# An edge tile of 672 bytes and the forgetting attention's two heads side by side, in a three-layer network

## The chip, the cores and the metric

One core of one Trainium2 chip runs the whole network in one launch. The metric is device time in microseconds, the median of three runs.

## The reference

512 tokens of width 1024 in float32 go through three layers. Layer one mixes with an RWKV recurrence, layer two with a gated convolution of 31 taps; both go on with cross attention to 256 memory tokens and with a feed-forward net with a short convolution (width 2 x 2816). Layer three is a hybrid of gated linear attention and forgetting attention, the part that the change rewrites:

```
h = rmsnorm_2(x, norm_mix_g)
gq, gk, gv, gr, glr, fq, fk, fv, ff, g_gla, g_fox = split(h @ w_in)
...
fqh, fkh = rmsnorm of fq, fk for each of 8 heads of 64
log_f = log_sigmoid(ff + fox_forget_b); c = cumsum(log_f over tokens)
for i in range(4):                       # query blocks of 128 tokens
    lo, hi = i * 128, (i + 1) * 128
    logits = q[lo:hi] @ k[:hi].T * 64**-0.5 + c[lo:hi, None] - c[None, :hi]
    p = softmax(where(causal, logits, -inf))
    out[lo:hi] = p @ v[:hi]
...
y = sigmoid(g_gla + gate_b[0]) * (o_gla @ w_gla_branch) + sigmoid(g_fox + gate_b[1]) * (o_fox @ w_fox_branch)
x = x + y @ w_out
```

## The kernel before

Activations stand with the 1024 channels on partitions, eight tiles of 128 x 512 tokens, float32. A dense product of float32 numbers is made from three float32r matmuls: weights and activations are split into a high part (rounded to float32r) and the rest, and `acc3` (L218 to L220) issues high x high, weight high x activation low, weight low x activation high for each of the 128-channel steps. An output tile of 128 channels x 512 tokens from 1024 input channels is so 24 matmuls of 512 columns, and one from 2816, as in the second product of a feed-forward net, 66: 24 from `bh` and `bl`, 24 from `h`, 18 from `mid`. The weights are read by SyncE's queue into `wr`, rounded by ScalarE into `wh` (L63) and the rest made by VectorE or GpSimd into `wl` (L64).

Tiles come from pools that the program lays out as two stacks in each partition of the on-chip memory. The left stack holds the weights, temporaries and the `home` tiles (`h0` and on, which hold `h` and, in the feed-forward nets, `mid`), and above them the pools of a stage. The right stack holds one pool, `act`, opened by `open_act` (L122 and on): `x` and the split activations `ah`, `al`, `bh`, `bl` (`slot`, `pair`), 2,048 bytes each. It begins at byte 229,344 and grows down. Pool `hy` of the hybrid stage begins with `aw2` and `fb` (L716), and all that this stage allocates later stands above.

In the hybrid stage the projections of forgetting attention for four pairs of heads, its attention itself and twenty output tiles of the two gates (`gates`, one tile being 24 float32r matmuls) are interleaved by hand. `fox_pair` (L945) is a generator; each `next` issues a step of the pair: the projection of q and k (L954, yields), the norms (L962 to L971, yields), then for each head the broadcast of its decay sums (L977 to L979), the scores of four query blocks (L984, on 64 rows of the array, since a head has 64 channels) with their softmax (L986 on VectorE, L988 on GpSimd, L990 on VectorE, L991 on ScalarE, L992 and L993 on VectorE), yields, then for each of four key blocks the transpositions of the probabilities (L1000), ScalarE's copy (L1003) and one value matmul over all the queries that see the key block (L1004, 64 output channels, 512 to 128 columns). A string for each pair, `FOX` (L1631), sets the order: `c` is the next step of the pair, `Q` the projection of the next pair, `n` the norms of the next pair, `G` one gate tile. Within its queue an engine runs in order; a scheduler places instructions by the program's text and dependences, and the engines wait for one another by semaphores. A float32 matmul, such as those of L984, L1000 or L1004, shows as two records in the trace unless it transposes.

Of the kernel before, what the change touches and what calls it, by code (L numbers as in the profile page):

```python
# [8 lines left out]
F32 = mybir.dt.float32  # L9
F32R = mybir.dt.float32r  # L10
AF = mybir.ActivationFunctionType
# [4 lines left out]
P = 128  # L16
T = 512
# [78 lines left out]
class Net:  # L96
    def __init__(self, ctx, tc, args, vec_at, order):
        self.ctx, self.tc, self.nc, self.a, self.vec_at = ctx, tc, tc.nc, args, vec_at
        nc = self.nc
        self.keep = ctx.enter_context(tc.tile_pool(name="keep", bufs=1))  # L100
        self.wpool = ctx.enter_context(tc.tile_pool(name="wts", bufs=1))
        self.tmp = ctx.enter_context(tc.tile_pool(name="tmp", bufs=1))
        self.hpool = ctx.enter_context(tc.tile_pool(name="home", bufs=1, reuse_waits="tile"))
        self.w = Weights(nc, self.wpool, [(k, self.wap(k)) for k in order])
        self.n = 0
        self.logs = False
        nv = args["vecs"].shape[1]
        self.vecs = self.keep.tile([P, nv], F32, name="vecs")
        self.consts()
# [597 lines left out]
    def hybrid(self, g_next):  # L707
        nc = self.nc
        mmul = nc.tensor.matmul
        with ExitStack() as ctx:  # L710
            pool = ctx.enter_context(self.tc.tile_pool(name="hy", bufs=1, reuse_waits="tile"))
            rs, rs_col = self.two_norms("final_g")
            xs, side = self.xs, self.side
            w2 = pool.tile([17, 256], F32, name="aw2")
            nc.sync.dma_start(out=w2, in_=self.a["gla_w2"])
            fb = pool.tile([P, 8], F32, name="fb")  # L716
            nc.sync.dma_start(out=fb, in_=self.a["fox_b"])

            def evict_rs(out, ps, n=T):
# [20 lines left out]
            with self.tc.tile_pool(name="hyt", bufs=1, reuse_waits="tile") as tp:  # L740
                self.chunk_consts(tp, True)

                ps = self.mm()
# [10 lines left out]
                for i in range(2):  # L754
                    ps = self.aux()
# [3 lines left out]
                    t = self.t512("u", 3)  # L759
# [14 lines left out]
                cq = pool.tile([P, 4, 8], F32, name="cq")  # L774
# [18 lines left out]
                for p in range(2):  # L793
# [10 lines left out]
                    ps = self.aux()  # L804
# [6 lines left out]
                for tb in range(4):  # L811
                    for p in range(2):
# [4 lines left out]
                        for h in range(2):  # L817
                            r = slice(h * 64, h * 64 + 64)
# [6 lines left out]
                            po = self.mm()  # L825
                            mmul(po[:, :P], lhsT=gv[tb][:, hh * P : (hh + 1) * P], rhs=sh, start=True, stop=(tb == 0), skip_group_check=True)
                            pos.append(po)
                        for c in range(2):
                            n = 2 * tb + c
                            if n:  # L830
                                for h in range(2):
                                    r = slice(h * 64, h * 64 + 64)
                                    o = c * 64
                                    mmul(pos[h][:, o : o + 64], lhsT=state[p][r, :], rhs=gqk[p][r, n * 64 : n * 64 + 64], start=False, stop=(c == 1),
                                         skip_group_check=True)
                            if n < 7:
                                kv = self.aux()
                                for h in range(2):
                                    r = slice(h * 64, h * 64 + 64)
                                    hh = 2 * p + h  # L840
                                    mmul(kv[r, :P], lhsT=kt[p][tb][c * 64 : c * 64 + 64, r], rhs=gv[tb][c * 64 : c * 64 + 64, hh * P : (hh + 1) * P],
                                         start=True, stop=True)
# [10 lines left out]
                ps = self.aux()  # L853
# [9 lines left out]
                for h in range(4):  # L863
                    b = self.bcast_tokens(y[:, :, h])
# [4 lines left out]
            with self.tc.tile_pool(name="hyf", bufs=1, reuse_waits="tile") as tp:  # L869
                fv = [tp.tile([P, 512], F32, name=f"fv{b}") for b in range(4)]  # L870
# [74 lines left out]
    def fox_pair(self, p, tp, xs, rs, cq, fv, of):  # L945
        nc = self.nc
        mmul = nc.tensor.matmul
        qk = {}

        def evict(m, ps):  # L950
            u = tp.tile([P, T], F32, tag="qk", bufs=4, name=self.nm("qk"))
            nc.vector.tensor_tensor(out=u, in0=ps, in1=rs, op=ALU.mult)
            qk[m // 4] = u

        self.linear("hy_fqk", KD, [p, 4 + p], lambda k: xs[k], evict, group=1)
        yield
        ps = self.aux()
        for i in range(2):
            s = self.t512("sq", 2)
            nc.scalar.activation(out=s, in_=qk[i], func=AF.Square)  # L960
            for tb in range(4):
                mmul(ps[:, tb * 4 + 2 * i : tb * 4 + 2 * i + 2], lhsT=s[:, tb * P : (tb + 1) * P], rhs=self.blk2, start=True, stop=True)  # L962
        v, y = self.small(16, "z"), self.small(16, "z")
        nc.vector.tensor_scalar(out=v, in0=ps[:, :16], scalar1=1.0 / 64, scalar2=1e-6, op0=ALU.mult, op1=ALU.add)
        self.rsqrt(y, v, 16)
        y4 = y.rearrange("p (a b) -> p a b", b=4)
        nc.vector.tensor_scalar(out=y4[:, :, 0:2], in0=y4[:, :, 0:2], scalar1=0.125, scalar2=None, op0=ALU.mult)
        rows = self.rows(y4, 4, tp)
        for i in range(2):
            b = self.pick(self.sel2, i, rows)  # L970
            nc.vector.scalar_tensor_tensor(out=qk[i], in0=qk[i], scalar=self.vec("fox_g", i), in1=b, op0=ALU.mult, op1=ALU.mult)  # L971
        yield
        po = None
        for h in range(2):
            hd = 2 * p + h
            r = slice(h * 64, h * 64 + 64)
            b = self.bcast_tokens(cq[:, :, hd])  # L977
            cb = tp.tile([P, T], F32, tag="cb", bufs=2, name=self.nm("cb"))
            nc.scalar.activation(out=cb, in_=b, func=AF.Copy)  # L979
            es = []  # L980
            for qb in range(4):
                n = (qb + 1) * P
                ps = self.aux()
                mmul(ps[:, :n], lhsT=qk[0][r, qb * P : n], rhs=qk[1][r, :n], start=True, stop=True)  # L984
                e = tp.tile([P, T], F32, tag="fe", bufs=4, name=self.nm("fe"))
                nc.vector.scalar_tensor_tensor(out=e[:, :n], in0=ps[:, :n], scalar=cq[:, qb, hd : hd + 1], in1=cb[:, :n], op0=ALU.add, op1=ALU.subtract)  # L986
                d = e[:, qb * P : n]
                nc.gpsimd.affine_select(out=d, in_=d, compare_op=ALU.is_ge, fill=-3.0e38, base=0, pattern=[[-1, P]], channel_multiplier=1)  # L988
                nm, sm = self.small(1, "c"), self.small(1, "c")
                nc.vector.tensor_reduce(out=nm, in_=e[:, :n], axis=AX.X, op=ALU.max, negate=True)  # L990
                self.last_exp = nc.scalar.activation(out=e[:, :n], in_=e[:, :n], func=AF.Exp, bias=nm, accum_out=sm).ins  # L991
                nc.vector.reciprocal(out=sm, in_=sm)  # L992
                nc.vector.tensor_scalar(out=e[:, :n], in0=e[:, :n], scalar1=sm, scalar2=None, op0=ALU.mult)  # L993
                es.append(e)
            yield
            po = po or self.mm()
            for kb in range(4):
                ps = self.aux()
                for qb in range(kb, 4):
                    nc.tensor.transpose(ps[:, (qb - kb) * P : (qb - kb + 1) * P], es[qb][:, kb * P : (kb + 1) * P], self.ident)  # L1000
                n = (4 - kb) * P
                t = tp.tile([P, T], F32, tag="fpt", bufs=3, name=self.nm("fpt"))
                nc.scalar.activation(out=t[:, :n], in_=ps[:, :n], func=AF.Copy)  # L1003
                mmul(po[r, kb * P :], lhsT=fv[kb][:, hd * 64 : hd * 64 + 64], rhs=t[:, :n], start=(kb == 0), stop=(kb == 3), skip_group_check=True)  # L1004
            if h == 0:
                yield
        nc.scalar.activation(out=of, in_=po, func=AF.Copy)
        yield
# [619 lines left out]
GATES = [4, 12, 5, 13, 6, 14, 7, 0, 1, 2, 3, 15, 8, 16, 9, 17, 10, 18, 11, 19]  # L1628
GLA_G = 2, 0, 1, 0, 1, 1, 0, 1, 0, 0

FOX = "cGQccncGGc", "GQccnGcGc", "GcQccnGGc", "GGcGGccGc"  # L1631


def hy_keys():
# [133 lines left out]
```

## Time and profile before

| | |
|---|---|
| median of three runs | 2687.13 us (2686.7 to 2687.75) |
| the profiled execution | 2691.29 us |
| its span | 2688.5 us |
| TensorE busy | 2581.6 us, 96% |
| weight loads (beside the matmuls) | 2000.3 us, 74% |
| VectorE, ScalarE, GpSimd busy | 54%, 40%, 14% |
| chain that ended last | TensorE 88%, VectorE 7% |
| forgetting attention's stretch | 2008 to 2235 us |

The span is the time from the first to the last instruction of the profiled execution; its own time has some 3 us around it. The page gives busy shares and groups of instructions; the timeline gives the start and the modelled duration of each matmul, so that the distance of two starts is a measurement and the duration is not.

### The profile page before, as it was taken

How to read it: one execution, taken by the hardware profiler on the slowest of the kernel's cores; microseconds unless marked ns; L12 is line 12 of the kernel's file. 1: busy time of each engine (PE TensorE's matmuls, PEld its weight loads, DVE VectorE, ACT ScalarE, POOL GpSimd, SP SyncE). 2: the span in 40 equal slices, each digit the busy share in tenths (PEclk: the TensorE clock that was granted, in tenths of full speed). 3: DMA queues.
4: the chain of work that ended last, by engine and by line, in shares of the span. 5: the costliest groups of instructions: out<-in, count | busy, mean ns of one | idle time of the engine just before them, and what ended most of it. 6: DMA issues, size and time to landing. Idle time of an engine off the chain costs nothing.

```text
span 2688.5 us, 33718 instructions
## 1 busy us (share of the span) xinstructions
PE 2581.6 (96%) x13436; PEld 2000.3 (74%) x13436; DVE 1463.5 (54%) x2140; ACT 1067.4 (40%) x1709; POOL 368.3 (14%) x362
## 2 busy tenths in 40 slices
PE   6987889899999999999999999999999999999998
PEld 5666767677888888765677888887786677888886
DVE  7584887745677733322654777534324456655522
ACT  6754355534444423312443444323223344433321
POOL 3037422430100001000202000001010000100000
PEclk9997569899999999999999999999998899999999
DMA  3211001321332233443311322232211113322232
GB/s 109 71 51 63 2 17 41 124 94 40 102 99 95 92 92 102 128 124 93 111 63 63 110 94 94 88 91 75 71 63 56 40 40 101 96 94 94 92 93 81
DMA packets 69596, 218.33 MB, mean 81 GB/s; under 512 B 9228, under 2 KB 14749, under 8 KB 69439
## 3 DMA queue, kind: packets, MB, share of 16 engines
q1 hardware_dynamic: 69438, 216.19, 25.6%
q8 instruction: 105, 1.72, 0.3%
q14 instruction: 53, 0.43, 0.1%
HBM read 205.69 MB, written 2.10 MB: 77 GB/s over the span
## 4 chain that ended last, share of the span: by engine, by line
PE 88%; DVE 7%; ACT 2%; POOL 2%; issue 1%; DMA 0%; DVEq 0%; POOLq 0%; ACTq 0%
PE mm L218 24%; PE mm L220 24%; PE mm L219 24%; PE aux L613 2%; PE mm L216 2%; PE aux L321 1%; PE mm L1004 1%; PE mm L1371 1%; POOL inv L1320 1%; POOL inv L1319 1%; PE aux L984 1%; DVE u L1159 1%; DVE h L1289 0%; DVE ml L246 0%; PE aux L1000 0%
## 5 line engine op out<-in xcount | busy, mean ns | idle before, releaser
L63 ACT ACTIVATE wh<-wr 128x1024 fp32r<-128x1024 f32 (+5 forms) x382 | 388.2, 1019 | 788.3 <-PE mm L219 629.0
L64 DVE TENSOR_TENSOR wl<-wr,wh 128x1024 fp32r<-128x1024 f32 (+3 forms) x341 | 401.7, 1179 | 294.8 <-ACT wh L63 292.5
L218 PE MATMUL mm<-ah,wh 128*128 128x512 f32 x1088 | 432.8, 398 | 0.9 <-ACT wh L63 0.9
L219 PE MATMUL mm<-al,wh 128*128 128x512 f32 x1088 | 431.2, 397 | 2.4 <-DVE al L246 2.4
L220 PE MATMUL mm<-ah,wl 128*128 128x512 f32 x1088 | 430.0, 397 | 0.6 <-DVE wl L64 0.5
L218 PE MATMUL mm<-bh,wh 128*128 128x512 f32 (+1 forms) x1000 | 399.7, 401 | 0.0
L219 PE MATMUL mm<-bl,wh 128*128 128x512 f32 (+1 forms) x1000 | 398.1, 398 | 0.0
L220 PE MATMUL mm<-bh,wl 128*128 128x512 f32 (+1 forms) x1000 | 396.6, 398 | 0.0
L218 PEld LDWEIGHTS mm<-ah,wh 128*128 128x128 f32 x1088 | 204.7, 188 | 54.2 <-ACT wh L63 3.7
L219 PEld LDWEIGHTS mm<-al,wh 128*128 128x128 f32 x1088 | 204.8, 188 | 52.8 <-DVE al L246 3.0
L220 PEld LDWEIGHTS mm<-ah,wl 128*128 128x128 f32 x1088 | 204.9, 188 | 50.9 <-DVE wl L64 2.3
L218 PEld LDWEIGHTS mm<-bh,wh 128*128 128x128 f32 (+1 forms) x1000 | 188.6, 189 | 49.9 <-issue 3.9
L269 POOL TENSOR_TENSOR acc<-acc,sq 128x512 f32<-128x512 f32 x55 | 88.3, 1605 | 1001.0 <-ACT sq L268 1000.6
L219 PEld LDWEIGHTS mm<-bl,wh 128*128 128x128 f32 (+1 forms) x1000 | 188.4, 188 | 48.1 <-issue 3.3
L220 PEld LDWEIGHTS mm<-bh,wl 128*128 128x128 f32 (+1 forms) x1000 | 188.1, 188 | 47.9 <-issue 1.7
L381 DVE TENSOR_TENSOR u<-mm,rs 128x512 f32<-128x512 f32 x132 | 90.9, 691 | 176.9 <-PE mm L220 176.7
L64 POOL TENSOR_TENSOR wl<-wr,wh 128x1024 fp32r<-128x1024 f32 (+2 forms) x41 | 98.9, 2413 | 589.6 <-ACT wh L63 589.3
L366 DVE TENSOR_TENSOR x<-x,mm 128x512 f32<-128x512 f32 x56 | 38.5, 687 | 138.8 <-PE mm L220 138.7
L219 PE MATMUL mm<-ml,wh 128*128 128x512 f32 (+1 forms) x224 | 91.4, 409 | 2.4 <-DVE ml L246 2.4
L218 PE MATMUL mm<-mh,wh 128*128 128x512 f32 (+1 forms) x224 | 87.7, 413 | 5.2 <-ACT mh L245 3.7
L220 PE MATMUL mm<-mh,wl 128*128 128x512 f32 (+1 forms) x224 | 90.1, 405 | 1.3 <-DVE wl L64 1.3
L395 ACT ACTIVATE uy<-uy 128x512 f32<-128x512 f32 x66 | 41.6, 632 | 122.5 <-DVE uy L393 122.4
(494 smaller groups left out, 4051.3 us busy)
## 6 DMA issues: line engine op xcount, KB each, us to landing
wr<-ffn_w_in SPq DMA_DIRECT2D x132, 512.0 KB, 3.4
wr<-ffn_w_out SPq DMA_DIRECT2D x48, 448.0 KB, 3.3
wr<-ffn_w_out SPq DMA_DIRECT2D x24, 512.0 KB, 3.5
wr<-hy_g SPq DMA_DIRECT2D x20, 512.0 KB, 3.5
wr<-kv_k SPq DMA_DIRECT2D x16, 512.0 KB, 3.5
wr<-kv_v SPq DMA_DIRECT2D x16, 512.0 KB, 3.5
wr<-xattn_w_q SPq DMA_DIRECT2D x16, 512.0 KB, 3.4
wr<-xattn_w_o SPq DMA_DIRECT2D x16, 512.0 KB, 3.4
```

Source lines behind the costliest of these rows:

```text
L63: self.last_hi = self.nc.scalar.activation(out=hi[:r, :c], in_=t[:r, :c], func=AF.Copy).ins
L64: (self.nc.gpsimd if i in W_POOL else self.nc.vector).tensor_tensor(out=lo[:r, :c], in0=t[:r, :c], in1=f32(hi[:r, :c]), op=ALU.subtract)
L216: self.last_mm = mm(out, lhsT=w[0], rhs=x[0], start=first, stop=last).ins
L218: mm(out, lhsT=w[0], rhs=x[0], start=first, stop=False)
L219: mm(out, lhsT=w[0], rhs=x[1], start=False, stop=False)
L220: mm(out, lhsT=w[1], rhs=x[0], start=False, stop=last)
L269: nc.gpsimd.tensor_tensor(out=self.sq, in0=self.sq, in1=s, op=ALU.add)
L321: self.last_bcast = self.nc.tensor.matmul(ps[:, b * P : (b + 1) * P], lhsT=col[:, b : b + 1].to_broadcast([P, P]), rhs=self.ident, start=T ...
L366: self.nc.vector.tensor_tensor(out=self.x[m], in0=self.x[m], in1=ps, op=ALU.add)
L381: nc.vector.tensor_tensor(out=u, in0=ps, in1=rs, op=ALU.mult)
L395: self.last_silu = nc.scalar.activation(out=y, in_=y, func=AF.Silu if l < 2 else AF.Gelu_apprx_tanh).ins
L613: nc.tensor.matmul(ps[32 * g : 32 * g + 32, 4 * e :], lhsT=w[:, 8 * g + e], rhs=t[:, g, : T - 4 * e], start=(e == 0), stop=(e == 7), skip_ ...
```

## The change

Four edits. A pool `edge` with one tile of 672 bytes is opened on the right side before all others; nothing reads or writes it. `fb` is allocated with 64 bytes where it had 32, and the same 32 are used. `fox_pair` makes both heads' broadcasts first, then goes by query block: the scores of a block for both heads back to back (`scores`, the heads on array rows 0 to 63 and 64 to 127), and one step later the transpositions, copies and value matmuls of that block for both heads (`values`, the heads on array columns 0 to 63 and 64 to 127, 128 query columns each). The strings of `FOX` are written anew for the new steps, with as many gate tiles in each.

```diff
@@ Net.__init__
         self.keep = ctx.enter_context(tc.tile_pool(name="keep", bufs=1))
+
+        ctx.enter_context(tc.tile_pool(name="edge", bufs=1, side="right")).tile([P, 168], F32, name="edge")
@@ hybrid
-            fb = pool.tile([P, 8], F32, name="fb")
+            fb = pool.tile([P, 16], F32, name="fb")[:, :8]
@@ fox_pair
+        heads = [(2 * p + h, slice(h * 64, h * 64 + 64)) for h in range(2)]
+        cbs = []
+        for hd, r in heads:
+            cb = tp.tile([P, T], F32, tag="cb", bufs=2, name=self.nm("cb"))
+            nc.scalar.activation(out=cb, in_=self.bcast_tokens(cq[:, :, hd]), func=AF.Copy)
+            cbs.append(cb)
         po = None
-        for h in range(2):
-            hd = 2 * p + h
-            r = slice(h * 64, h * 64 + 64)
-            b = self.bcast_tokens(cq[:, :, hd])
-            cb = tp.tile([P, T], F32, tag="cb", bufs=2, name=self.nm("cb"))
-            nc.scalar.activation(out=cb, in_=b, func=AF.Copy)
+
+        def scores(qb):
+            n = (qb + 1) * P
+            pss = [self.aux() for _ in heads]
+            for ps, (hd, r) in zip(pss, heads):
+                mmul(ps[:, :n], lhsT=qk[0][r, qb * P : n], rhs=qk[1][r, :n], start=True, stop=True)
             es = []
-            for qb in range(4):
-                n = (qb + 1) * P
-                ps = self.aux()
-                mmul(ps[:, :n], lhsT=qk[0][r, qb * P : n], rhs=qk[1][r, :n], start=True, stop=True)
+            for ps, cb, (hd, r) in zip(pss, cbs, heads):
                 e = tp.tile([P, T], F32, tag="fe", bufs=4, name=self.nm("fe"))
...
                 es.append(e)
-            yield
-            po = po or self.mm()
-            for kb in range(4):
+            return es
+
+        def values(qb, es):
+            n = (qb + 1) * P
+            ts = []
+            for e in es:
                 ps = self.aux()
-                for qb in range(kb, 4):
-                    nc.tensor.transpose(ps[:, (qb - kb) * P : (qb - kb + 1) * P], es[qb][:, kb * P : (kb + 1) * P], self.ident)
-                n = (4 - kb) * P
+                for kb in range(qb + 1):
+                    nc.tensor.transpose(ps[:, kb * P : (kb + 1) * P], e[:, kb * P : (kb + 1) * P], self.ident)
                 t = tp.tile([P, T], F32, tag="fpt", bufs=3, name=self.nm("fpt"))
                 nc.scalar.activation(out=t[:, :n], in_=ps[:, :n], func=AF.Copy)
-                mmul(po[r, kb * P :], lhsT=fv[kb][:, hd * 64 : hd * 64 + 64], rhs=t[:, :n], start=(kb == 0), stop=(kb == 3), skip_group_check=True)
-            if h == 0:
+                ts.append(t)
+            for kb in range(qb + 1):
+                for t, (hd, r) in zip(ts, heads):
+                    mmul(po[r, n - P : n], lhsT=fv[kb][:, hd * 64 : hd * 64 + 64], rhs=t[:, kb * P : (kb + 1) * P], start=(kb == 0), stop=(kb == qb),
+                         skip_group_check=True)
+
+        last = None
+        for qb in range(5):
+            es = scores(qb) if qb < 4 else None
+            if qb:
+                po = po or self.mm()
+                values(qb - 1, last)
+            last = es
+            if qb < 4:
                 yield
@@ the strings
-FOX = "cGQccncGGc", "GQccnGcGc", "GcQccnGGc", "GGcGGccGc"
+FOX = "ccGcQcGcnGc", "cGcQcGcnGc", "cGcQcGcnGc", "cGcGcGcGGc"
```

The order on TensorE at the first pair of heads, before: the four scores of one head (L984, scores into `aux` from the normalised q and k), then all ten transpositions (L1000, of the probabilities `fe`), then the first value matmul (L1004; `fpt` the copied probabilities, `fv` the values). The rows give line, output, moving operand or operands, and size.

```order
L984 MATMUL aux_15549<-qk_15398,qk_15365 128x128
L984 MATMUL aux_15562<-qk_15398,qk_15365 128x256
L984 MATMUL aux_15575<-qk_15398,qk_15365 128x384
L984 MATMUL aux_15588<-qk_15398,qk_15365 128x512
L1000 MATMUL aux_15602<-ident,fe_15551 128x128
L1000 MATMUL aux_15602<-ident,fe_15564 128x128
L1000 MATMUL aux_15610<-ident,fe_15564 128x128
L1000 MATMUL aux_15602<-ident,fe_15577 128x128
```

At the same place, after: scores (now L988) of both heads in turn, two blocks, then the transpositions (now L1009) of the first block, two more scores, a value matmul (now L1015), and a gate tile begins (L220 to L222).

```order
L988 MATMUL aux_15461<-qk_15402,qk_15369 128x128
L988 MATMUL aux_15462<-qk_15402,qk_15369 128x128
L988 MATMUL aux_15520<-qk_15402,qk_15369 128x256
L988 MATMUL aux_15521<-qk_15402,qk_15369 128x256
L1009 MATMUL aux_15547<-ident,fe_15465 128x128
L1009 MATMUL aux_15551<-ident,fe_15476 128x128
L988 MATMUL aux_15623<-qk_15402,qk_15369 128x384
L988 MATMUL aux_15624<-qk_15402,qk_15369 128x384
L1015 MATMUL mm_15546<-fpt_15549,fv_15204 64x128
L220 MATMUL mm_15557<-bh_13525,wh_15490 128x512
L221 MATMUL mm_15557<-bl_13526,wh_15490 128x512
```

The eight scores of two heads, which stood in two runs of four, now stand in pairs, and a block's transposition stands right behind the scores of two blocks.

The value matmuls of the first pair's second head, before: each of the four has its own size, with the scores of the next head between them.

```order
L1004 MATMUL mm_15601<-fpt_15799,fv_15200 64x512
L321 MATMUL aux_15919<-ident,cq 128x128 x4
L1004 MATMUL mm_15601<-fpt_15806,fv_15201 64x384
L984 MATMUL aux_15926<-qk_15540,qk_15507 128x128
L1004 MATMUL mm_15601<-fpt_15812,fv_15202 64x256
L984 MATMUL aux_15939<-qk_15540,qk_15507 128x256
L1004 MATMUL mm_15601<-fpt_15817,fv_15203 64x128
L984 MATMUL aux_15952<-qk_15540,qk_15507 128x384
```

The value matmuls of the first pair's third block and fourth block are now runs of pairs; this is the third block, after: heads in turn (two `fpt`), three key blocks (`fv`), 128 columns each.

```order
L1015 MATMUL mm_15546<-fpt_15725,fv_15204 64x128
L1015 MATMUL mm_15546<-fpt_15731,fv_15204 64x128
L1015 MATMUL mm_15546<-fpt_15725,fv_15205 64x128
L1015 MATMUL mm_15546<-fpt_15731,fv_15205 64x128
L1015 MATMUL mm_15546<-fpt_15725,fv_15206 64x128
L1015 MATMUL mm_15546<-fpt_15731,fv_15206 64x128
```

What was one matmul of 512, 384, 256 or 128 columns for each head and key block is now one of 128 columns for each head, query block and key block, with the other head's directly behind it.

## Rows read from the trace of the kernel before

**Rows 1.** The page, section 4: chain that ended last, by engine and line.

```profile
PE 88%; DVE 7%; ACT 2%; POOL 2%; issue 1%; DMA 0%; DVEq 0%; POOLq 0%; ACTq 0%
PE mm L218 24%; PE mm L220 24%; PE mm L219 24%; PE aux L613 2%; PE mm L216 2%; PE aux L321 1%; PE mm L1004 1%; PE mm L1371 1%; POOL inv L1320 1%; POOL inv L1319 1%; PE aux L984 1%; DVE u L1159 1%; DVE h L1289 0%; DVE ml L246 0%; PE aux L1000 0%
```

**Rows 2.** The page, section 5: line, names, shapes, count; busy, mean ns; idle.

```profile
L218 PE MATMUL mm<-ah,wh 128*128 128x512 f32 x1088 | 432.8, 398 | 0.9 <-ACT wh L63 0.9
...
L218 PE MATMUL mm<-bh,wh 128*128 128x512 f32 (+1 forms) x1000 | 399.7, 401 | 0.0
```

**Rows 3.** TensorE's timeline: start us, duration us, out<-moving,weights, rows*columns of the array.

```profile
953.00 0.40 PE L218 MATMUL mm<-h,wh 128*128 128x512 f32 x1
...
962.80 0.40 PE L218 MATMUL mm<-bh,wh 128*128 128x512 f32 x1
...
968.40 0.39 PE L218 MATMUL mm<-h,wh 128*128 128x512 f32 x1
...
978.01 0.40 PE L218 MATMUL mm<-bh,wh 128*128 128x512 f32 x1
```

**Rows 4.** TensorE's timeline, an output tile made from yh and yl.

```profile
2286.18 0.40 PE L218 MATMUL mm<-yh,wh 128*128 128x512 f32 x1
...
2291.78 0.40 PE L218 MATMUL mm<-yh,wh 128*128 128x512 f32 x1
```

**Rows 5.** TensorE's timeline, the key and value product.

```profile
482.22 0.40 PE L218 MATMUL mm<-wh,mnh 128*128 128x512 f32 x1
...
487.82 0.63 PE L218 MATMUL mm<-wh,mnh 128*128 128x512 f32 x2
```

**Rows 6.** TensorE's timeline in a stretch at half clock.

```profile
2042.29 0.63 PE L220 MATMUL mm<-bh,wl 128*128 128x512 f32 x1
2042.71 0.61 PE L218 MATMUL mm<-bh,wh 128*128 128x512 f32 x1
```

**Rows 7.** Windows: stretch, us, busy of each engine (instructions), granted clock, DMA, GB/s.

```profile
2008.00:2235.00 227.00, 218.68 (x915) 151.36 (x915) 109.24 (x234) 88.09 (x179) 11.61 (x34) 0.94 0.16 50
2029.50:2043.20 13.70, 13.15 (x39) 8.07 (x40) 3.25 (x14) 3.25 (x10) 0.00 (x0) 0.50 0.00 0
2084.10:2091.00 6.90, 5.00 (x14) 2.18 (x14) 3.36 (x12) 3.40 (x10) 0.29 (x1) 0.51 0.00 1
```

**Rows 8.** TensorE's timeline, first pair; in brackets idle time before and who ended it.

```profile
2025.17 2.42 PE L984 MATMUL aux<-qk,qk 64*128 64x128 f32 x8 [0.36 <-DVE qk L971]
2029.47 0.46 PE L1000 MATMUL aux<-ident,fe 128*128 128x128 f32 x1 [1.89 <-DVE fe L993]
2030.44 2.42 PE L1000 MATMUL aux<-ident,fe 128*128 128x128 f32 x9 [0.51 <-DVE fe L993]
```

**Rows 9.** TensorE's timeline, row tiles of 64 and column tiles of 32.

```profile
386.45 1.16 PE L1371 MATMUL mm<-zr,h 64*128 64x128 f32 x16
...
1133.91 6.89 PE L613 MATMUL aux<-cu,cw 128*32 128x512 f32 x64
```

**Rows 10.** TensorE's timeline, two records of a value matmul of 128 columns.

```profile
2081.40 0.43 PE L1004 MATMUL mm<-fpt,fv 128*64 128x128 f32 x2
```

**Rows 11.** Waits, 2008 to 2235 us: who for whom, us, times, longest.

```profile
PE aux L1000 <- DVE fe L993: 7.3, 6, 1.9
```

**Rows 12.** Groups on ScalarE, 2008 to 2235 us.

```profile
L1003 ACT ACTIVATE fpt<-aux 128x128 f32<-128x128 f32 x8 | 2.2, 278 | 8.6 <-PE mm L1004 6.8 <-PE aux L1000 1.6
```

**Rows 13.** Groups on TensorE, 2008 to 2235 us, forms together.

```profile
L1004 PE MATMUL mm<-fpt,fv 128*64 128x512 f32 (+3 forms) x64 | 26.4, 519 | 0.7 <-ACT fpt L1003 0.4
L984 PE MATMUL aux<-qk,qk 64*128 64x128 f32 (+3 forms) x64 | 23.1, 465 | 0.4 <-DVE qk L971 0.4
```

**Rows 14.** Groups on VectorE, 2008 to 2235 us, blocks of 512 columns.

```profile
L986 DVE SCALAR_TENSOR_TENSOR fe<-aux,cq,cb 128x512 f32<-128x512 f32 x8 | 6.0, 746 | 0.1
...
L990 DVE TENSOR_REDUCE c<-fe 128x1 f32<-128x512 f32 x8 | 5.4, 670 | 0.0
...
L993 DVE TENSOR_SCALAR fe<-fe,c 128x512 f32<-128x512 f32 x8 | 3.9, 486 | 0.2
```

## The prediction

> **What bounds the kernel now.** I read the chain of work that ended last first [rows 1]: 88% of the span is TensorE, and the three lines of the split product, L218, L219 and L220, make 72%. So what counts is how fast the float32r matmuls of 512 columns follow one another, and where TensorE stops. For the first I read the starts of single matmuls in TensorE's timeline; a mean duration doesn't serve, since its end is modelled and overlaps the next (398 and 401 ns in [rows 2] at starts 230 ns apart). For the second I read the stretch of the forgetting attention, 2008 to 2235 us, by windows, timeline and waits.
>
> What the starts show: an output tile of a feed-forward net's second product has 24 matmuls that read bh and bl, then 42 that read h and mid. The 24 take 968.40 - 962.80 = 5.60 us [rows 3], 233.3 ns each, the 42 take 978.01 - 968.40 = 9.61 us, 228.8 ns each. Output bank, weight buffers, shapes, types and clock are the same. What differs is where the moving operand lies: in the built program h and mid start at multiples of 64 bytes, while ah, al, bh, bl (and x) start 32 bytes past one, because the right-hand stack ends at byte 229,344 and every tile in it is 2,048 bytes. It isn't the high address: yh and yl lie at byte 108,128, on the left, also 32 past, and run at (2291.78 - 2286.18) / 24 = 233.3 ns [rows 4]. Two things speak against the reading: of 24 such output tiles (three layers), one ran at the slow spacing with h and mid too (953.00 to 962.80, 42 in 9.80 us [rows 3]), and the key and value product, whose moving operand wh starts at a multiple of 64, runs at (487.82 - 482.22) / 24 = 233.3 as well [rows 5].
>
> **Part 1, the edge tile and fb.** 672 bytes are ten and a half times 64, so every tile of the right-hand stack moves to a multiple of 64; fb grows by 32 bytes and moves every later tile of the hybrid stage, yh, yl, qk, fe and fpt among them, to one too. No instruction is added, and up to the forgetting attention the order on every engine is unchanged. The program has 7,028 float32r matmuls of 512 columns whose moving operand is 32 past; the first and largest groups are [rows 2] and their kind on L219 and L220. 6,831 of them are followed without a gap at full clock; at half clock starts lie 420 ns apart (2042.29 to 2042.71, [rows 6]), which hides 4.5 ns. 6,831 x (233.3 - 228.8) ns = 30.7 us. Since one aligned run in 24 ran at the slow spacing, and seams where another operation comes between give nothing, I take nine tenths: **27 us**. Bounds: nothing (if the cause is another) and 31 us. What the move does to VectorE, ScalarE or DMA no row shows; they have 54%, 40% and a quarter of the span, so I take nothing, and 3 us either way.
>
> **Part 2, heads side by side.** The stretch takes 227 us, TensorE 218.68 of it [rows 7]. One head's scores are four matmuls on 64 rows, 8 records of 128 to 512 columns, 2,560 columns in 2.42 us [rows 8], 0.945 ns a column; eight heads make 19.4 us. A head's values are four matmuls on 64 columns with the same 2,560 columns in records, so 19.4 us again. Now the two heads of a pair lie back to back on the two halves of the array. Do such halves run side by side? L1371, 64-row tiles in both halves: 16 records of 128 columns in 1.16 us, 0.57 ns a column. L613, four column tiles of 32: 64 records of about 512 columns in 6.89 us, 0.21 ns a column [rows 9]. So columns halve or better and rows fall to 0.5 to 0.6. By halves 19.4 us are saved of 38.8; by 0.6 on both, 15.5.
>
> Against it: the values become 80 matmuls of 128 columns where 32 were, 96 more records. Two records of 128 columns stand in 0.43 us [rows 10] where 256 x 0.945 would be 0.24; the other 0.19 is the modelled tail once, or 0.1 us for each record, so 96 records cost between nothing and, two abreast, 5 us; the halves of L1371 show little of it, and I take 1. In the order the first value matmul of a pair's first block stands alone, thirteen gate matmuls before its partner: four pairs lose 0.24 us, 1 us. Changes between whole-array and part-array matmuls fall from 90 to 78, a gain too small to count. Together 19.4 - 1 - 1 = 17.4 us.
>
> The Trainium skill, "TensorEngine Tiling (Array Packing)", section "Instruction Overhead", states some 60 cycles of overhead for each matmul, against splitting one into several. As an estimate by that page, 96 records of 60 cycles at 2.4 GHz are 2.4 us, and the sum would be 1 to 2 us later; no row here shows it by itself.
>
> **Part 3, waits.** Before, three times the same stop: TensorE issues the last score of a head and has nothing until VectorE has normalised the first block (1.89 us, then 0.51 us more [rows 8]), 7.3 us in all by the waits [rows 11]. Each is followed by a stretch at half clock, 13.7 us at 0.50 and 6.9 at 0.51 [rows 7], and a third like the second at 2138.7. In the new order a gate (24 x 0.233 = 5.6 us) or a projection stands between a block's softmax and its transpositions, but not at the first block of a pair: there the first transposition comes right after the scores of two blocks. That is late next. From first score to first transposition it is 4.3 us now (2025.17 to 2029.47 [rows 8]); the cover is 2 heads x 384 columns x 0.945 = 0.7 us in pairs 0 and 3, and 0.8 us more in pairs 1 and 2, where seven values of the pair before stand between. So the wait is at most 3.6 and 2.8 us, and at least nothing; VectorE had a split of weights and three other blocks in its queue in those 4.3 us, and now has one other block. Half way, and ScalarE's two copies of 0.28 us before the first value [rows 12]: 2 x 1.8 + 2 x 1.4 + 4 x 0.56 = 8.6 us, 1.3 more than what goes. Queued behind each on TensorE is a gate, for which nobody waits. Against that, scores and values fill 26.4 + 23.1 = 49.5 us of TensorE now [rows 13], 10.7 more than their 38.8: single value matmuls wait between single scores for their copies, or run at half clock. In the new order a block's values come in one run behind a gate; I let that give back the 1.3, so the waits come to nothing net, with -8 (all four at their most) and +7 (none) as bounds. The half clock of before costs half of TensorE's busy time in those stretches, (13.15 + 2 x 5.00) / 2 = 12 us; four stops of some 2 us may set it off as three of 2.4 did, so I take it as unchanged, with -12 and +7. ScalarE, VectorE and POOL do the same instructions on the same sizes; the transpositions (80) and the copies (32) keep their number.
>
> **Sum.** 27 + 17.4 + 0 = 44.4. The profiled execution took 2691.29 us, its span 2688.5, the median of the runs is 2687.13; the sum is made on the profiled one, 2691.3 - 44.4 = 2646.9, and the 4.2 us by which it lies over the median come off again: **2643 us**.
>
> **Rivals.** R1, the address does nothing: what makes 233.3 is something else that goes with the tiles a and b. For it: the aligned run at 233.3 and the key and value product [rows 3, 5]. Against it: 23 of 24 runs, and yh on the other side of the memory. Then only part 2 remains: 2687 - 17 = 2670; if half the matmuls profit, 2656. The Trainium skill, "SBUF — State Buffer", section "Specifications (TRN2)", gives a cacheline of 16 bytes for the memory; by that rule 32 and 64 are both on a line's start, and R1 would hold. The 228.8 and 233.3 of the same weights speak against it, and no run here has yet moved a tile.
>
> R2, the halves don't run side by side, because matmuls alternate heads with a weight load before each, on fp32 that goes through in two records: the change doesn't do what it says. Against: L1371 and L613 do just that. Then 17 us fall away: 2687 - 27 = 2660. R1 and R2 together give 2687.
>
> R3, slower: the softmax of two heads doesn't fit behind a gate. VectorE needs for a head's 512-column block 746 + 670 + 486 ns [rows 14] and a reciprocal, 2.1 us, for two heads 4.1, and beside it the gates' evictions and the split of weights wait on the same engine. Each of 16 steps would then stop TensorE for 2.4 us, 13 more than now, 31 us, and be followed by 6.9 us at half clock, 13 x 6.9 / 2 = 45: 2687 + 31 + 45 - 17 - 27 = 2719. It decides once chain and queue exceed 5.6 us at more than about half the steps. Against: smaller blocks need less, and VectorE is busy 109.24 of 227 us [rows 7].
>
> **How the numbers follow.** Forecast (2622 to 2650): 0.62. Half of R1 (2656): 0.10. R1 (2670): 0.12. R2 (2660): 0.09. Both (2687): 0.03. R3 (2719): 0.04. 0.2% is 5.4 us, about what a measurement of this kernel can tell from no change: faster 0.93, same 0.03, slower 0.04. Low end: 31 for part 1, 20 for part 2, the half clock's 12 and 2 of the waits, 2687 - 65 = 2622; the high end takes in R1 with 2 us, 2672, and leaves out what lies above, about a tenth.
>
> **What would show it.** Right, step by step: 24 matmuls from bh, ah or yh take 5.49 us (24 x 228.8); pairs of L988 and L1015 (the new lines of scores and values) at about half the time; the three waits of 1.89 us gone, one of 1 to 4 us before the first transposition of each pair; the stretch near 227 - 17 - 3 = 207 us, where 3 is its part of the 27. Wrong: 24 matmuls still in 5.60 us (R1); values and scores at 0.9 ns a column (R2); waits of the transpositions for VectorE in most steps and a clock near 0.5 through much of the stretch (R3).

## The result and the profile after

The changed kernel takes 2655.19 us (median of four runs, 2653.71 to 2658.22) against 2687.44 us (of four runs too), a ratio of 0.988 with a 95% interval of 0.9863 to 0.9897: 32 us faster, inside the stated range, 12 us slower than the 2643 us forecast. The profiled execution took 2655.39 us, so it lies at the median, where the one of before lay 4 us over its own: of the 34.9 us by which the traces differ, some 3 are that.

The page of the changed kernel, its span, TensorE's busy time, its granted clock in 40 slices, and the chain by engine and line, to be held against [rows 1]:

```profile
span 2653.6 us, 33923 instructions
...
PE 2539.1 (96%) x13532; PEld 2003.1 (75%) x13532; DVE 1462.4 (55%) x2140; ACT 1067.9 (40%) x1709; POOL 369.6 (14%) x362
...
PEclk9997568899999999999999999999988999999999
...
PE 88%; DVE 6%; ACT 2%; POOL 2%; issue 1%; DMA 1%; DVEq 0%; POOLq 0%; ACTq 0%
PE mm L220 25%; PE mm L222 25%; PE mm L221 24%; PE aux L615 2%; PE mm L218 2%; PE aux L323 1%; PE mm L1391 1%; POOL inv L1339 1%; POOL inv L1340 1%; PE mm L1015 1%; ACT wh L63 1%; DVE h L1309 0%; PE aux L988 0%; PE aux L1009 0%; PE aux L1291 0%
```

The bound hasn't moved: 88% of the chain is TensorE, the same three lines (now L220 to L222) 74%. The span is 34.9 us shorter, and where it went is read off by laying the same matmul of both traces side by side (their order on TensorE is the same but for the attention's stretch). At the stretch's beginning (2008.07 us before, 1989.94 after) the changed kernel is 18.1 us ahead; in the stretch it gains 11.1 (227.1 us before, 216.0 after); from there to the end 5.6 more.

**The placement.** TensorE's timeline, the first matmul of two output tiles made from ah and al, 24 matmuls apart:

```profile
2303.07 0.39 PE L220 MATMUL mm<-ah,wh 128*128 128x512 f32 x1
...
2308.56 0.39 PE L220 MATMUL mm<-ah,wh 128*128 128x512 f32 x1
```

5.49 us, 228.8 ns each, as forecast; [rows 3] had 5.60. But not all that was moved to a multiple of 64 got faster. Two starts 24 matmuls apart of an output tile from yh and yl, which lie at such a multiple now:

```profile
2255.69 0.39 PE L220 MATMUL mm<-yh,wh 128*128 128x512 f32 x1
...
2261.29 0.39 PE L220 MATMUL mm<-yh,wh 128*128 128x512 f32 x1
```

Still 5.60 us, as in [rows 4]. The first layer's mixed operands also stayed at 233 ns. So a multiple of 64 isn't the rule.

**The stretch of the forgetting attention.** Windows of the changed kernel (stretch, length, busy of TensorE, weight loads, VectorE, ScalarE, GpSimd, then the granted clock), the whole stretch and two of its five pieces at half clock (the windows' edges take in a little of what lies beside):

```profile
1990.00:2206.00 216.00, 198.22 (x1012) 151.46 (x1011) 110.04 (x234) 87.79 (x180) 13.37 (x34) 0.94 0.16 52
1994.90:2005.20 10.30, 7.07 (x28) 5.33 (x28) 3.91 (x12) 1.78 (x3) 0.20 (x1) 0.52 0.18 52
2008.60:2012.00 3.40, 3.40 (x10) 1.97 (x11) 2.25 (x6) 0.98 (x5) 0.42 (x2) 0.56 0.00 0
```

TensorE is busy 20.5 us less than in [rows 7] (198.22 for 218.68), but the stretch is only 11 us shorter: idle time went from 8.3 to 17.8 us. Half clock takes 23.9 us in five pieces, where it took 27.3 in three. The groups on TensorE in the stretch (busy, mean ns, idle before and who ended it), to be held against [rows 13]:

```profile
L1015 PE MATMUL mm<-fpt,fv 128*64 128x128 f32 x160 | 15.6, 287 | 0.7 <-ACT fpt L1011 0.7
L988 PE MATMUL aux<-qk,qk 64*128 64x128 f32 (+3 forms) x64 | 14.3, 503 | 0.0
L1009 PE MATMUL aux<-ident,fe 128*128 128x128 f32 x80 | 13.4, 294 | 7.1 <-DVE fe L999 5.4 <-DVE c L998 1.6
L323 PE MATMUL aux<-ident,cq 128*128 128x128 f32 x64 | 12.6, 371 | 0.0
...
L1585 PE MATMUL aux<-row,sel 64*128 64x512 f32 x8 | 3.4, 510 | 6.5 <-DVE row L248 6.5
L1040 PE MATMUL aux<-ident,rp 128*32 128x128 f32 x16 | 2.8, 306 | 3.5 <-DVE rp L1036 3.5
```

Values (L1015) and scores (L988) fill 15.6 + 14.3 = 29.9 us where they filled 49.5. That is 19.6 us, for which the forecast had 17.4. What takes half of it back stands in the waits of TensorE in the stretch (us in total, times, longest), against 7.3 for the one row of [rows 11]:

```profile
PE aux L1585 <- DVE row L248: 6.5, 4, 2.5
...
PE aux L1009 <- DVE fe L999: 5.4, 5, 2.2
...
PE aux L1040 <- DVE rp L1036: 3.5, 1, 3.5
...
PE aux L1009 <- DVE c L998: 1.6, 1, 1.6
...
PE mm L1015 <- ACT fpt L1011: 0.7, 2, 0.4
```

Together 17.7 us. The waits of the transpositions, L1009, for VectorE are 7.0 us in all, forecast 6.4 without the copies. The other 10.0 us stand at the norms: L1040 transposes the norm's row, and L1585 is the matmul that spreads it. TensorE waited for neither before. The timeline shows the waits, at the first pair and the beginning of the second:

```profile
1996.74 1.01 PE L1040 MATMUL aux<-ident,rp 128*32 128x128 f32 x4 [3.45 <-DVE rp L1036]
1999.14 1.22 PE L1585 MATMUL aux<-row,sel 64*128 64x512 f32 x2 [1.39 <-DVE row L248]
2000.29 3.78 PE L323 MATMUL aux<-ident,cq 128*128 128x128 f32 x16
2004.00 2.13 PE L988 MATMUL aux<-qk,qk 64*128 64x128 f32 x8
2007.74 0.30 PE L1009 MATMUL aux<-ident,fe 128*128 128x128 f32 x1 [1.61 <-DVE c L998]
2008.24 0.33 PE L1009 MATMUL aux<-ident,fe 128*128 128x128 f32 x1 [0.19 <-DVE fe L999]
...
2045.31 0.60 PE L1040 MATMUL aux<-ident,rp 128*32 128x128 f32 x4
2048.37 0.73 PE L1585 MATMUL aux<-row,sel 64*128 64x512 f32 x2 [2.46 <-DVE row L248]
```

TensorE waits 3.45 us for VectorE's work on the norm's row, 1.39 more for its split, and falls to half clock; then 1.61 us for the first block's softmax, as forecast. At the second pair there are 2.46 us between L1040 and L1585, and the same again at the third.

The same place at the first pair before, where the two were L1020 and L1565; of the twelve gate matmuls between them, the rows of eleven are left out:

```profile
2019.68 0.60 PE L1020 MATMUL aux<-ident,rp 128*32 128x128 f32 x4
2020.03 0.48 PE L218 MATMUL mm<-bh,wh 128*128 128x512 f32 x1
...
2023.00 0.72 PE L1565 MATMUL aux<-row,sel 64*128 64x512 f32 x2
```

TensorE has work for all of the 3.3 us from one to the other, and stops at neither.

### The profile page after: what moved, and what is told of

It reads as the page before. It is cut to its first block, busy times and chain, and to the rows that moved or that the text cites. A ratio compares the mean times of both kernels' runs of the same rounds, so it can differ in the third digit from the quotient of the medians.

```text
span 2653.6 us, 33923 instructions
## 1 busy us (share of the span) xinstructions
PE 2539.1 (96%) x13532; PEld 2003.1 (75%) x13532; DVE 1462.4 (55%) x2140; ACT 1067.9 (40%) x1709; POOL 369.6 (14%) x362
## 4 chain that ended last, share of the span: by engine, by line
PE 88%; DVE 6%; ACT 2%; POOL 2%; issue 1%; DMA 1%; DVEq 0%; POOLq 0%; ACTq 0%
PE mm L220 25%; PE mm L222 25%; PE mm L221 24%; PE aux L615 2%; PE mm L218 2%; PE aux L323 1%; PE mm L1391 1%; POOL inv L1339 1%; POOL inv L1340 1%; PE mm L1015 1%; ACT wh L63 1%; DVE h L1309 0%; PE aux L988 0%; PE aux L1009 0%; PE aux L1291 0%
## 5 line engine op out<-in xcount | busy, mean ns | idle before, releaser
L222 PE MATMUL mm<-ah,wl 128*128 128x512 f32 x1088 | 427.8, 395 | 0.5 <-DVE wl L64 0.5
L220 PE MATMUL mm<-ah,wh 128*128 128x512 f32 x1088 | 426.4, 393 | 1.2 <-ACT wh L63 1.1
L220 PE MATMUL mm<-bh,wh 128*128 128x512 f32 (+1 forms) x1000 | 395.1, 396 | 0.2
L222 PE MATMUL mm<-bh,wl 128*128 128x512 f32 (+1 forms) x1000 | 393.2, 395 | 0.0
L220 PEld LDWEIGHTS mm<-ah,wh 128*128 128x128 f32 x1088 | 204.7, 188 | 50.5 <-ACT wh L63 4.0
L222 PEld LDWEIGHTS mm<-ah,wl 128*128 128x128 f32 x1088 | 204.8, 188 | 43.9 <-DVE wl L64 2.3
L222 PEld LDWEIGHTS mm<-bh,wl 128*128 128x128 f32 (+1 forms) x1000 | 188.2, 188 | 43.7 <-issue 1.0
L220 PEld LDWEIGHTS mm<-bh,wh 128*128 128x128 f32 (+1 forms) x1000 | 188.0, 188 | 42.3 <-ACT wh L63 1.5
L220 PE MATMUL mm<-mh,wh 128*128 128x512 f32 (+1 forms) x224 | 87.6, 413 | 5.4 <-ACT mh L247 3.7
L222 PE MATMUL mm<-mh,wl 128*128 128x512 f32 (+1 forms) x224 | 90.0, 404 | 1.3 <-DVE wl L64 1.3
```

Of the source, the lines that this page charges most:

```text
L220: mm(out, lhsT=w[0], rhs=x[0], start=first, stop=False)
L222: mm(out, lhsT=w[1], rhs=x[0], start=False, stop=last)
```

## The experiments

Each is timed against the kernel before, measured beside it: at 2689.3 us for the edge tile alone, the 608 bytes, the moved weights and the heads alone; at 2689.0 for the distances 0 and 256, the neighbouring values and the norms; at 2687.8 for distance 0 without the heads and for both. Changed lines stand alone, without those around them.

**The edge tile alone.**

```diff
+        ctx.enter_context(tc.tile_pool(name="edge", bufs=1, side="right")).tile([P, 168], F32, name="edge")
```

> The kernel before with the edge tile of 672 bytes alone; heads and fb as before. Theory A (a moving operand at a multiple of 64 bytes lets 24 float32r matmuls follow in 5.49 us instead of 5.60): the trace of the changed kernel is 18.1 us ahead where the forgetting attention begins and gains 5.6 us behind it, so about 25 us less than the kernel before, near 2662 us. R1 (the address does nothing): 2687 us. The forgetting attention's stretch stays at 227 us but for 2 us.

2661.4 us, 0.9896 (0.9881 to 0.9911), 28 us less. The trace is 28.0 us shorter over the whole program. R1 is out: the place of a tile that nobody reads is worth most of the change.

**608 bytes instead of 672**, against the run before it.

```diff
-        ctx.enter_context(tc.tile_pool(name="edge", bufs=1, side="right")).tile([P, 168], F32, name="edge")
+        ctx.enter_context(tc.tile_pool(name="edge", bufs=1, side="right")).tile([P, 152], F32, name="edge")
```

> The same with an edge tile of 608 bytes: the right-hand tiles lie at multiples of 128 bytes, where 672 put them 64 past one. The weights lie at multiples of 128 in both. Theory A (multiples of 64 suffice): the same 25 us, near 2662 us. Theory B (the moving operand must lie 64 past a multiple of 128, as h and mid did before, while yh at a multiple of 128 stayed at 233 ns after the change): 24 matmuls from ah or bh still take 5.60 us and the time stays at 2687 us.

2683.1 us, 0.9974 (0.9964 to 0.9985): 6 us, not 28. The first matmuls of two tiles from ah, 48 matmuls apart in its trace:

```profile
2327.59 0.39 PE L220 MATMUL mm<-ah,wh 128*128 128x512 f32 x1
...
2338.75 0.39 PE L220 MATMUL mm<-ah,wh 128*128 128x512 f32 x1
```

11.16 / 48 = 232.5 ns. So the theory on which I forecast part 1 falls: a multiple of 64, even of 128, doesn't suffice. And at the same edge the first layer's mixed operands, which had stayed at 233 under 672 bytes, ran at 227.4.

**The weights moved instead**, in the changed kernel, as in the two runs that follow.

```diff
-        ctx.enter_context(tc.tile_pool(name="edge", bufs=1, side="right")).tile([P, 168], F32, name="edge")
+        ctx.enter_context(tc.tile_pool(name="edge", bufs=1, side="right")).tile([P, 136], F32, name="edge")
...
+        ctx.enter_context(tc.tile_pool(name="gapa", bufs=1)).tile([P, 16], F32, name="gapa")
         self.wpool = ctx.enter_context(tc.tile_pool(name="wts", bufs=1))
+        ctx.enter_context(tc.tile_pool(name="gapb", bufs=1)).tile([P, 16], F32, name="gapb")
```

> The changed kernel with the split weights 64 bytes further on (a 64-byte tile ahead of their pool and one behind it; the edge tile 128 bytes smaller, so that all other tiles lie as in the changed kernel modulo 128). Moving operands ah, bh, h and mid and the weights now lie 64 past a multiple of 128 both. Theory A (the moving operand's address alone, multiples of 64): as the changed kernel, 2655 us. Theory B1 (the moving operand alone, 64 past a multiple of 128): also 2655 us. Theory B2 (moving operand and weights must lie in different halves of 128 bytes): 24 matmuls in 5.60 us again, h and mid too, near 2655 + 30 = 2685 us, and yh, at a multiple of 128, at 5.49.

2680.4 us, 0.9968 (0.9957 to 0.9978): 25 us of the gain are gone, though the moving operands lie as before modulo 128. Two tiles, 48 matmuls apart:

```profile
2325.42 0.40 PE L222 MATMUL mm<-ah,wh 128*128 128x512 f32 x1
...
2336.57 0.40 PE L222 MATMUL mm<-ah,wh 128*128 128x512 f32 x1
```

11.15 / 48 = 232.3 ns, and h and mid, at 228.9 in every other run until then, are at 232.5 too. It is the distance from moving operand to weights that counts. But a mere "other half of 128 bytes" (B2) isn't it either, since the first layer's operands, at the same 64 as their weights, ran at 227.7. All spacings so far fitted one table by the distance modulo 512: 0, 320, 384 and the rest.

**Distance 0** (i1_same512).

```diff
-        ctx.enter_context(tc.tile_pool(name="edge", bufs=1, side="right")).tile([P, 168], F32, name="edge")
+        ctx.enter_context(tc.tile_pool(name="edge", bufs=1, side="right")).tile([P, 120], F32, name="edge")
...
         self.wpool = ctx.enter_context(tc.tile_pool(name="wts", bufs=1))
+        ctx.enter_context(tc.tile_pool(name="gapb", bufs=1)).tile([P, 48], F32, name="gapb")
```

> The changed kernel with every large moving operand at the same place as the weights modulo 512 bytes: an edge tile of 480 bytes instead of 672 and a tile of 192 bytes behind the weights on the left. In the runs so far the spacing of float32r matmuls of 512 columns goes by the distance (moving operand less weights) modulo 512: 0 (some 240 matmuls of the first layer, edge 608) 227.4 ns, 320 228.9, 384 232.4, every other one 233.3. If that holds, ah, bh, h and mid, 7,000 matmuls, go from 228.9 to 227.4: 10 us under the changed kernel, near 2645 us; yh goes from 233.3 to 228.9. If the 227.4 belonged to the first layer's stage and not to the distance: 2655 us, as the changed kernel.

2635.3 us, 0.9805 (0.9789 to 0.982): 20 us better than the changed kernel. Two tiles, 48 matmuls apart:

```profile
2291.16 0.39 PE L221 MATMUL mm<-ah,wh 128*128 128x512 f32 x1
...
2302.04 0.39 PE L221 MATMUL mm<-ah,wh 128*128 128x512 f32 x1
```

10.88 / 48 = 226.7 ns, less than the 227.4 expected, for ah, bh, h and mid alike; the yh tiles went to 229.1, as distance 320 foretold, and the first layer's, now at 128, to 232.5. The key and value product of [rows 5] lies at distance 0 here too, with the parts exchanged: there the split weights `wh` are the moving operand and `mnh` is what is loaded. It had 5.60 us for 24 matmuls at distance 192, and has 5.47 now, 227.9 ns:

```profile
480.07 0.40 PE L221 MATMUL mm<-wh,mnh 128*128 128x512 f32 x1
...
485.54 0.62 PE L221 MATMUL mm<-wh,mnh 128*128 128x512 f32 x2
```

**Distance 256.**

```diff
-        ctx.enter_context(tc.tile_pool(name="edge", bufs=1, side="right")).tile([P, 168], F32, name="edge")
+        ctx.enter_context(tc.tile_pool(name="edge", bufs=1, side="right")).tile([P, 56], F32, name="edge")
```

> The changed kernel with an edge tile of 224 bytes: ah and bh lie 256 past the weights modulo 512; h and mid stay at 320. If what counts is the distance modulo 256, this is distance 0 and they take 227.4 ns, some 9 us under the changed kernel, near 2646 us. If it is the distance modulo 512, 256 is a new place and, like most, 233.3: 24 matmuls in 5.60 us, near 2682 us.

2638.5 us, 0.9821 (0.9798 to 0.9844). Two tiles, 48 matmuls apart:

```profile
2286.37 0.39 PE L220 MATMUL mm<-ah,wh 128*128 128x512 f32 x1
...
2297.25 0.39 PE L220 MATMUL mm<-ah,wh 128*128 128x512 f32 x1
```

226.7 ns again: the period is 256 bytes, not 512. (h and mid, left at 320, stay near 229.)

**Distance 0 without the heads.** The placement of the run "Distance 0" (i1_same512) in the kernel before, two lines more and nothing else.

> The kernel before with the placement of i1_same512 alone (edge tile of 480 bytes, 192 bytes behind the weights), heads and strings as before. If the spacing goes by the distance modulo 256 (226.7 ns at distance 0, where it was 233.3): 6.6 ns for the 6,234 matmuls from ah and bh and 2.2 ns for the 993 from h and mid that run without gaps, 41 + 2 = 43 us, near 2645 us. If the heads side by side are what lets the better placement show: near 2660 us, as with the edge tile of 672.

2644.8 us, 0.9841 (0.9825 to 0.9858), on the expected 2645. Placement alone, two tiles of bytes that nobody reads, beats the changed kernel by 10 us.

**The heads side by side alone**, no edge tile, fb at 32 bytes.

> The changed kernel without the edge tile and with fb at 32 bytes: the heads side by side alone. If the two parts add up, what the trace of the changed kernel shows for the stretch, 11 us less with some 2 us of that from the address: 9 us less than before, near 2678 us; my forecast was 17 less, 2670 us. 24 matmuls from bh still in 5.60 us.

2679.1 us, 0.9968 (0.9955 to 0.9981): 10 us. In the trace its stretch is 8.4 us shorter, with the same waits at the norms (6.5 and 3.4 us). Whether the two parts of the change add up is not shown: the product of their ratios, 0.9896 x 0.9968 = 0.9864, lies at the lower end of the interval measured (0.9863 to 0.9897), and 6 us of their 38 are not in its 32. At distance 0 they do add up: 0.9841 x 0.9968 = 0.9810 for a measured 0.9805 (0.9789 to 0.982).

**Neighbouring values on the same columns.**

```diff
-            for kb in range(qb + 1):
-                for t, (hd, r) in zip(ts, heads):
+            for t, (hd, r) in zip(ts, heads):
+                for kb in range(qb + 1):
```

> The changed kernel with the value matmuls of a block in another order: all key blocks of one head, then all of the other, so that neighbours lie on the same array columns. If neighbours on different columns run side by side and others don't, the value matmuls take 160 records x 128 columns x 0.945 ns = 19.4 us and more where they now take 14.0: 5 to 9 us over the changed kernel, 2660 to 2664 us. If the order of the heads doesn't matter: 2655 us.

2667.4 us, 0.9919 (0.9897 to 0.994), 12 us over the changed kernel, more than either theory said. Runs of value matmuls in the changed kernel, 14 records of a fourth block and 12 of a third:

```profile
2054.24 1.09 PE L1015 MATMUL mm<-fpt,fv 128*64 128x128 f32 x14
...
2083.94 0.88 PE L1015 MATMUL mm<-fpt,fv 128*64 128x128 f32 x12
```

The same with the heads one after the other, 16 and 12:

```profile
2052.49 1.58 PE L1015 MATMUL mm<-fpt,fv 128*64 128x128 f32 x16
...
2085.62 1.14 PE L1015 MATMUL mm<-fpt,fv 128*64 128x128 f32 x12
```

Within runs at full clock the starts are 64 ns apart on average with heads in turn and 81 with heads apart. The single starts show more than the average. With heads in turn, one record of each head starts within 7 ns, and the next two 109 ns after them. With heads apart, the records of one head start 109 ns apart but for the first, so neighbours on the same columns follow one after the other; the second and third record of the 16 above (each row takes in the record after it):

```profile
2052.65 0.38 PE L1015 MATMUL mm<-fpt,fv 128*64 128x128 f32 x2
2052.76 0.38 PE L1015 MATMUL mm<-fpt,fv 128*64 128x128 f32 x2
```

The average is below 109 because, by the order of the program, the second head's first four records start beside the first head's last four; in a second block, with four records for each head, all overlap as they do with heads in turn. So order matters, and neighbours on the other columns run beside each other, but the values explain only 160 x 17 ns = 2.7 of the 12 us. The rest is clock and waits: the stretch's granted clock is 0.90 where it was 0.94, half clock takes 44.4 us where it took 23.9, and TensorE is idle 21.9 us where it was 17.8.

```profile
1990.00:2217.00 227.00, 205.10 (x1001) 156.77 (x1000) 109.44 (x234) 87.74 (x179) 9.68 (x34) 0.90 0.15 48
```

Why the clock stayed low longer isn't settled, and it can't be put down to the order of the heads alone: with heads in turn, the trace of "Distance 0" has 41.1 us of half clock in the same stretch.

```profile
1973.50:2195.00 221.50, 204.12 (x1011) 155.20 (x1010) 110.07 (x234) 87.73 (x179) 13.38 (x34) 0.91 0.16 51
```

**The norms one step earlier.**

```diff
-FOX = "ccGcQcGcnGc", "cGcQcGcnGc", "cGcQcGcnGc", "cGcGcGcGGc"
+FOX = "cGcQccnGcGc", "cGcQcnGcGc", "cGcQcnGcGc", "cGcGcGcGGc"
```

> The changed kernel with other strings: cGcQccnGcGc, cGcQcnGcGc, cGcQcnGcGc, cGcGcGcGGc. The norms of the next pair come one step earlier, and in TensorE's order 12 to 26 gate matmuls now stand between the transposition of the norm's row (L1040) and the matmul that spreads it (L1585), where none stood. Theory (of the stretch's new idle time, the four waits around the norms, 3.6 + 2.7 + 2.7 + 1.7 us, are half): those waits go, up to 10 us, and the transpositions of a pair's last block, which lose their gate, wait in their place for VectorE, some 2 us each: 2 to 8 us under the changed kernel, 2647 to 2653 us. If a stop only moves to wherever gates are taken from: 2655 us, no change.

2649.3 us, 0.9855 (0.9838 to 0.9871). TensorE's waits in the stretch:

```profile
PE aux L1009 <- DVE fe L999: 13.4, 7, 2.7
...
PE mm L1015 <- ACT fpt L1011: 2.7, 7, 0.6
```

The waits at L1040 and L1585 are gone, all 10 us, and those of the transpositions went from 7.0 to 13.4, those of the values from 0.7 to 2.7. The sum is 16.1 us for 17.7. The same matmuls show 0.3 us of gain in the stretch, and what else its execution is ahead was there before it; the two intervals overlap. So the stop only moves: gate tiles (G in the strings) are what covers it, and there are fourteen.

**Both.** The run "Distance 0" (i1_same512) with fb at 256 bytes, so that yh lies at distance 0 as well, and with these strings (v2_strings).

> The kernel i1_same512 with fb at 256 bytes, so that yh and yl lie at distance 0 too, and with the strings of v2_strings. 192 matmuls from yh at 226.7 for 228.9 ns: 0.4 us. If the strings save what the medians of v2_strings and of the changed kernel differ by: 6 us under i1_same512, 2629 us. If, as the waits of the two traces have it (17.8 us before, 16.4 after), the stops only move: 2634 us.

2634.5 us, 0.9803 (0.9788 to 0.9818): as i1_same512, not 6 us less. That agrees with the waits and not with the medians of v2_strings. It is the fastest kernel here, though nothing separates it from i1_same512. Their two traces are 8.8 us apart, nearly all of it in the stretch, where half clock takes 17 us in this one and 41.1 in the other: one execution's half clock can outweigh what the strings do, so single traces don't decide between two such kernels.

## Why the prediction was right, and where it wasn't

**Part 1: right in size by luck, wrong in its reason.** 27 us were forecast; the edge tile alone gave 28, and in the trace of the change 18.1 + 5.6 us lie outside the stretch. The forecast was right because 672 bytes put ah and bh at the same distance from the weights, 320 modulo 512, that h and mid had by chance, the tiles whose 228.8 ns I had read; any reason that makes them equal gives the same sum. By the reason given, 608 bytes would have been as good, and they gave 6 us. The step "what differs is where the moving operand lies ... at multiples of 64 bytes" named one address where there are two. Of the two exceptions that the prediction kept as evidence for R1, one pointed there: the key and value product of [rows 5] lay at a distance, 192, at which other tiles take 233.3 too, and fell to 227.9 at distance 0. For yh the step failed outright: no gain, 0.9 us of the 27. The other exception, the run of h and mid at 233.3 [rows 3], isn't explained by distance; in the changed kernel two output tiles from bh, begun at 1849.75 and 1893.73 us, run at 233.3 as well. What makes a run fall into the slow rhythm there is open.

**R1 was wrong as a whole**, its chance of 0.12 (and 0.10 for half) went to nothing. That 2655 us lies at the 2656 of "half of R1" is chance: the edge tile gave all its 27, and the norms took 10 back. The Trainium skill, "SBUF — State Buffer", section "Specifications (TRN2)", has cachelines of 16 bytes; were they the only grain of placement, no shift here would count. The 233.3, 232.4, 228.9 and 226.7 ns of these runs, all at multiples of 16, differ from that, and the measurement decides.

**Part 2: right.** 17.4 us forecast, 19.6 less busy time of values and scores. R2 is out: records of a pair start some 7 ns apart. The 1 us for the 96 records more doesn't show: 128 columns of both heads take 109 ns, where the sum had 0.945 x 128 = 121 for one head alone, since its 0.945 took in the modelled end of the last record.

**Part 3: the step that failed.** "So the waits come to nothing net", with 8 us more as the bound; TensorE's idle time in the stretch grew by 9.5. The four waits before a pair's first transposition came as forecast, 7.0 us where 6.4 were taken and 12.8 were the most. What the sum lacks is the other end of a pair: "That is late next" looked only from the scores on. In the order before, 12 to 32 gate matmuls stood between the transposition of the norm's row (L1020, now L1040) and the matmul that spreads it (L1565, now L1585); in the order after none do in three pairs and five in the fourth, and the excerpt shown ahead of the prediction begins behind them. With their 10.0 us the sum would have been 2643 + 10 = 2653 us; measured were 2655. The half clock, forecast as unchanged, was 23.9 us for 27.3, worth under 2 us.

**R3** named the right danger at the wrong place: transpositions didn't wait in each step, only at the first block of a pair, and most of the stop stood at the norms, where no gate was left between. The run with the norms one step earlier (v2_strings) shows the mechanism of it: a covered wait uncovers another.

## What to carry to other kernels

When the same instruction shows two rhythms in one trace, list the addresses of all its operands, not of one, and move one tile by bytes that nobody uses before giving a reason; the cheapest experiment here was worth more than the rewritten attention. A prediction from the order must follow each chain over the whole step, from the first instruction that lost its cover, since filler work is finite and here a gap closed at one place opened at another (10.0 us at the norms gone, 8.4 more elsewhere).

## What the runs showed of the hardware

The spacing of dense float32r matmuls of 512 columns at full clock, weights loaded for each, goes by the distance from weights to moving operand modulo 256 bytes: 226.7 ns at 0 (i1_same512, d256), 228.9 at 64 (the changed kernel), 232.4 or 233 at 128 (e2_edge608, e4_weights64), 233.3 at 32 (the yh tiles of i0_place), 96 and 224 (the kernel before) and 192 (the first layer of the changed kernel). A few output tiles at 64 ran at 233.3 all the same. Other distances weren't tried, and which part of the weight load and the moving read meet isn't shown.

Float32 matmuls of 128 columns on different halves of the array's columns start 7 ns apart and run side by side (the changed kernel); on the same half their records start 109 ns apart (h1_heads_outer).
